# A third chunk pair of the MLP's up projection as seven block products, with four raw weight buffers in place of two and a descriptor scratch of 8 KB for GpSimd

## The chip, the cores and the metric

The kernel runs on one core of a Trainium2 chip. The metric is the device time of one execution in microseconds (us), the median of several runs. Five engines work side by side and wait for one another by semaphores: TensorE (PE, matrix products; its weight loads are listed as PEld), VectorE (DVE), ScalarE (ACT), GpSimd (POOL) and SyncE (SP), whose queue issues most of the loads here. SBUF is the working memory on the chip, PSUM the memory into which TensorE writes.

## What is computed

A trunk of two layers on a sequence of 512 positions with 1024 channels, in float32. Each layer has a wide input projection, three branches (a gated recurrence, a spatial gating unit, a windowed attention), a gated merge and an output projection, and then the part that matters here:

```python
D_FF = 4 * D_MODEL
...
        hn = rms_norm(x, ln2[l])
        x = x + jnp.square(jax.nn.relu(hn @ w_up[l])) @ w_down[l]
```

`w_up` has 1024 x 4096 elements in a layer, `w_down` 4096 x 1024.

## The kernel before

**Products in three passes.** A float32 product is made of three passes of TensorE on a shorter format: each operand is split into hi (a cast on ScalarE) and lo (the difference, on VectorE), and hi by hi, hi by lo and lo by hi are added up in PSUM. `wsplit` (L201 to L205) does that for a weight chunk of 128 x 1024: L203 on ScalarE, L204 on VectorE. The split chunks lie in `wh` and `wl`, three buffers each (`WB`). `mm3` (L207 to L210) issues the three passes. `split` (L255 to L262) is the same for other tiles: L258 on ScalarE, L259 on VectorE.

**Weights.** All weights come in chunks of 512 KB. `wload` (L179) loads one into a raw buffer `wr` by SyncE's queue (L184) and splits it; there are two raw buffers (`WR`), used all over the kernel: by the projections of the branches, the merge, the output projection and the up chunks. `uload` (L187, the load at L193) loads eight chunks of one unit into the eight `wq` buffers (`NQ`).

**The MLP.** It is cut into four quarters `qd` of 1024 hidden channels (L1244). A quarter has an up half, eight chunks `f` in four pairs `j`, and a down half. A chunk of the up half is made in one of two ways:

- directly (`proj`, L1263): 8 blocks of the contraction times three passes, 24 matmuls of 512 columns; then ReLU and square on ScalarE (L1269, L1270).
- as a pair of two chunks (`up_pair`, L493 to L544): the pair is a 2 x 2 block product, and seven products of half the size replace eight. Each of the seven has 4 blocks times three passes, 12 matmuls of 256 columns (L522 to L524), in the order 1, 2, 6, 7, 5, 4, 3. Before them VectorE makes sums of the raw weights (L499, L500, L503, L505), one of them in a PSUM tile `t2`, and four splits follow from these (three of 1024 columns, and one of 512 columns out of `t2`). After them the partial results are copied and added (L527 to L537), then ReLU and square (L538 to L543). The sums of the activations, `hx`, are made once for a layer by `left_x` (L407).

Which pairs go which way stands in two tuples, one entry for a quarter: the pairs in `PAIRS` load into `wr` (L488, L489, `ahead` False), those in `AHEAD` load into `wq` before the quarter's other work. Quarter 0 has none. Quarters 1 to 3 have pair 1 in `AHEAD` and pair 2 in `PAIRS`; pairs 0 and 3 are direct.

The result of each chunk pair is prepared for the down half, by either way: `left_first` (L360) and `left_second` (L368) with `left_sums` (L375) make splits and sums of it (L365, L382, L383, L398, and splits at L258 and L259).

The down half (`down`, L471, by `seven`, L422) is the same trick on larger blocks: seven products P1, P2, P6, P7, P5, P4, P3, each of two weight chunks with 24 matmuls of 512 columns in all at L433 to L435 (two blocks of the contraction to each chunk, two output tiles, three passes, and so 12 matmuls to a chunk). Before the products 6, 5 and 4 VectorE adds raw chunks (L447, L449, L451); after each product it adds what is in PSUM to the rows of x (L478). In front stands one more sum of raw chunks (L420). The first product takes both PSUM banks of the tag "c", one for each output tile; each pair of the up half takes one of them in turn.

**Order.** The order of the instructions on each engine is fixed when the kernel is built: a scheduler takes what is ready in its own model of time, by priority. From L831 on `hp()` raises the priority of loads, splits and sums; within that, the order of the program counts. The matmuls of TensorE may be moved against each other in this way too, within what the data allow.

**GpSimd** issues the transfers that go through DRAM: gates and merged rows that are put aside and fetched again, and the residual rows. Their descriptors lie in a scratch in SBUF, 16384 bytes of each partition unless the kernel says otherwise.

Of the kernel before, what the change touches and what calls it, by code (L numbers as in the profile page):

```python
# [59 lines left out]
def trunk(tc, xT, xt, ws, vec, fnb, bsb, snk, wst, rope, cmask, amask, ident, out):  # L60
    nc = tc.nc
# [24 lines left out]
    HOME = {t: p for p, ts in {"G": ("xs", "zt"), "Y1": ("yh",), "br": ("q", "a", "g", "ch"), "Y2": ("yi", "th"), "mlp": ("h", "xm")}.items() for t in ts}  # L86
    part = {}
    BANKS = {"m": 2, "a": 2, "c": 2, "s": 2}
    PAIRS, AHEAD = ((), (2,), (2,), (2,)), ((), (1,), (1,), (1,))
    GROUPS = (("m", "m", "c", "c"), ("a", "a", "s", "s"))  # L90
    WR, WB, NZ, NSM, NQ = 2, 3, 2, 3, 8

    CTS = {2: 5, 3: 4}

# [1325 lines left out]
```

## Time and profile before

| | us |
|---|---|
| median of 3 runs | 1645.81 |
| lowest, highest run | 1644.52, 1646.40 |
| span of the profiled execution | 1644.4 |
| first up matmul of layer 0, last of layer 1 (start) | 495.0, 1597.9 |

The mean granted clock of TensorE in the profiled execution is 0.999 of full speed. The span goes from the first to the last instruction of the program. In the lines of the profile, a group reads: line, engine, operation, written tile <- read tiles, shape, count, then the busy time, the mean in ns, and the idle time of the engine just before with what ended it. In an order of time a line reads: start in us, duration in us, engine, line, operation, and in brackets the idle time before. A matmul's duration overlaps the next one's: its pace is read from start to start.

### The profile page before, as it was taken

The numbers are of one execution on the slowest core, as the hardware profiler recorded it, in microseconds if no ns is written. First come the engines' busy times: TensorE is split into PE (matmuls) and PEld (weight loads), VectorE is DVE, ScalarE is ACT, GpSimd is POOL, SyncE is SP. The second block draws the span as 40 slices with busy tenths as digits, with TensorE's granted clock in tenths as the row PEclk, the third lists the DMA queues.
The fourth block names the chain that finished last, engine by engine and source line by source line (L and its number), as shares of the span: only waits on it lengthen the run. The fifth ranks groups of instructions, "written<-read, shape, count | busy, mean of one in ns | idle before, by whom it ended". The sixth has DMA issues, their size and how long they took to land. (4 is left out here: it accounts for less than half of the span.)

```text
span 1644.4 us, 24323 instructions
## 1 busy us (share of the span) xinstructions
PE 1631.2 (99%) x9137; PEld 1376.8 (84%) x9137; DVE 1358.9 (83%) x2183; ACT 1012.9 (62%) x1731; POOL 102.4 (6%) x165
## 2 busy tenths in 40 slices
PE   9999999999999999999999999999999999999998
PEld 7788888888888898989888888888887888989896
DVE  7888979677758988898989869887877589898887
ACT  7667567677247564646666555886862464647374
POOL 0012000000300000000010110000003000000001
PEclk9999999999999999999999999999999999999999
DMA  8343222222625333232423432223226343232311
GB/s 309 102 154 125 78 90 73 102 97 85 236 92 190 100 106 103 103 115 91 141 90 125 144 121 78 77 91 105 92 86 232 106 162 117 89 128 77 129 65 52
DMA packets 55590, 191.55 MB, mean 116 GB/s; under 512 B 7376, under 2 KB 7632, under 8 KB 55472
## 3 DMA queue, kind: packets, MB, share of 16 engines
q1 hardware_dynamic: 44352, 154.43, 27.3%
q0 software_dynamic: 10688, 35.00, 5.8%
q8 instruction: 72, 1.18, 0.3%
q10 hardware_dynamic: 432, 0.55, 0.1%
q14 instruction: 46, 0.38, 0.1%
HBM read 173.18 MB, written 16.78 MB: 116 GB/s over the span
## 5 line engine op out<-in xcount | busy, mean ns | idle before, releaser
L203 ACT CAST wh<-wq 128x1024 fp32r<-128x1024 f32 x214 | 225.2, 1053 | 205.1 <-PE dA L434 60.9
L204 DVE TENSOR_TENSOR wl<-wq,wh 128x1024 fp32r<-128x1024 f32 x214 | 260.4, 1221 | 62.8 <-ACT wh L203 60.3
L203 ACT CAST wh<-wr 128x1024 fp32r<-128x1024 f32 x164 | 172.0, 1049 | 155.1 <-PE wo L251 27.5
L204 DVE TENSOR_TENSOR wl<-wr,wh 128x1024 fp32r<-128x1024 f32 x164 | 199.9, 1220 | 61.0 <-ACT wh L203 55.1
L210 PE MATMUL up<-xh,wl 128*128 128x512 f32 x320 | 124.8, 390 | 0.0
L209 PE MATMUL up<-xl,wh 128*128 128x512 f32 x320 | 124.8, 390 | 0.0
L208 PE MATMUL up<-xh,wh 128*128 128x512 f32 x320 | 124.6, 391 | 0.0
L434 PE MATMUL dA<-wh,sh 128*128 128x512 f32 x256 | 99.8, 390 | 0.0
L433 PE MATMUL dA<-wh,sh 128*128 128x512 f32 x256 | 98.5, 390 | 0.0
L435 PE MATMUL dA<-wl,sh 128*128 128x512 f32 x256 | 91.9, 389 | 0.0
L656 DVE TENSOR_TENSOR ex<-ex 128x512 f32<-128x512 f32 x112 | 74.9, 686 | 3.5 <-ACT kt L647 3.2
L208 PEld LDWEIGHTS up<-xh,wh 128*128 128x128 f32 x320 | 60.1, 188 | 12.4
L210 PEld LDWEIGHTS up<-xh,wl 128*128 128x128 f32 x320 | 60.1, 188 | 12.3
L209 PEld LDWEIGHTS up<-xl,wh 128*128 128x128 f32 x320 | 60.1, 188 | 12.2
L644 ACT ACTIVATE qt<-ex 128x512 f32<-128x512 f32 x56 | 37.9, 677 | 33.8 <-DVE ex L656 31.8
L433 PEld LDWEIGHTS dA<-wh,sh 128*128 128x128 f32 x256 | 48.1, 188 | 10.0
L434 PEld LDWEIGHTS dA<-wh,sh 128*128 128x128 f32 x256 | 48.1, 188 | 9.9
L435 PEld LDWEIGHTS dA<-wl,sh 128*128 128x128 f32 x256 | 48.1, 188 | 9.9
L523 PE MATMUL us<-xs,wh 128*128 128x256 f32 x192 | 54.1, 283 | 0.0
L522 PE MATMUL us<-xs,wh 128*128 128x256 f32 x192 | 54.1, 283 | 0.0
L524 PE MATMUL us<-xs,wl 128*128 128x256 f32 x192 | 53.4, 283 | 0.0
L208 PE MATMUL gz<-xh,wh 128*128 128x512 f32 x128 | 50.9, 398 | 0.0
(435 smaller groups left out, 4780.6 us busy)
## 6 DMA issues: line engine op xcount, KB each, us to landing
wr<-in_ws_dram SPq DMA_DIRECT2D x158, 512.0 KB, 3.5
wq<-in_ws_dram SPq DMA_DIRECT2D x124, 512.0 KB, 4.3
thd<-zt POOLq DMA_DIRECT2D x32, 256.0 KB, 2.5
gt<-thd POOLq DMA_DIRECT2D x32, 256.0 KB, 3.9
mgd<-mg POOLq DMA_DIRECT2D x16, 256.0 KB, 2.3
mB<-mgd POOLq DMA_DIRECT2D x16, 256.0 KB, 6.7
x<-in_xT_dram SPq DMA_DIRECT2D x8, 256.0 KB, 7.5
xt<-in_xt_dram SPq DMA_DIRECT2D x8, 256.0 KB, 8.3
```

The source lines that it names most:

```text
L203: nc.scalar.copy(hi, raw)
L204: nc.vector.tensor_tensor(lo, raw, hi.bitcast(F32), ALU.subtract)
L208: nc.tensor.matmul(pt, whi, xhi, start=first, stop=False)
L209: nc.tensor.matmul(pt, whi, xlo, start=False, stop=False)
L210: nc.tensor.matmul(pt, wlo, xhi, start=False, stop=last)
L433: nc.tensor.matmul(pt, xh[:, t], hi[:, c], start=start and k == 0, stop=False, skip_group_check=True)
L434: nc.tensor.matmul(pt, xl[:, t], hi[:, c], start=False, stop=False, skip_group_check=True)
L435: return nc.tensor.matmul(pt, xh[:, t], lo[:, c], start=False, stop=k == 3, skip_group_check=True)
L522: nc.tensor.matmul(pt, hi[:, c], xh, start=n in (1, 2, 7) and k == 0, stop=False, skip_group_check=True)
L523: nc.tensor.matmul(pt, hi[:, c], xl, start=False, stop=False, skip_group_check=True)
L524: nc.tensor.matmul(pt, lo[:, c], xh, start=False, stop=k == 3, skip_group_check=True)
L656: nc.vector.tensor_tensor(o_ap, o_ap, ap_of(ex, i_, [[istep, 2]] + z), ALU.add)
```

## The change

Three constants. Pair 3 (f = 6 and 7) of quarters 1 to 3 joins pair 2 in `PAIRS`, in both layers, so that three of the four pairs of these quarters are seven-product pairs. The raw weight buffers `wr` go from two to four, for all that use them; a buffer takes 4096 bytes of each partition. The scratch for GpSimd's descriptors goes from 16384 to 8192 bytes of each partition.

```diff
-    PAIRS, AHEAD = ((), (2,), (2,), (2,)), ((), (1,), (1,), (1,))
+    PAIRS, AHEAD = ((), (2, 3), (2, 3), (2, 3)), ((), (1,), (1,), (1,))
     GROUPS = (("m", "m", "c", "c"), ("a", "a", "s", "s"))
-    WR, WB, NZ, NSM, NQ = 2, 3, 2, 3, 8
+    WR, WB, NZ, NSM, NQ = 4, 3, 2, 3, 8
...
-    nc = _bacc.Bacc("TRN2", target_bir_lowering=False, num_devices=1)
+    nc = _bacc.Bacc("TRN2", target_bir_lowering=False, num_devices=1, dynamic_dma_scratch_size=8192)
```

## The prediction

> **What bounds the kernel now.** I read the page first, then the waits of TensorE, then windows of one quarter of the MLP, and last the order of time on TensorE and VectorE in that quarter. From the page:
>
> ```profile
> span 1644.4 us, 24323 instructions
> PE 1631.2 (99%) x9137; PEld 1376.8 (84%) x9137; DVE 1358.9 (83%) x2183; ACT 1012.9 (62%) x1731; POOL 102.4 (6%) x165
> ```
>
> From the waits of TensorE, its two longest (us in total, times, longest):
>
> ```profile
> PE idle L167 <- DVE idle L164: 1.6, 1, 1.6
> PE tA L435 <- DVE wl L204: 1.3, 1, 1.3
> ```
>
> TensorE works 1631.2 of 1644.4 us and hardly ever waits; nothing else sets the end. The kernel gets shorter by as much as TensorE is given less to do, provided that whoever feeds it keeps up. The windows (core busy times PE, PEld, DVE, ACT, POOL, then clock, DMA share, GB/s): two long stretches outside the MLP, then the up half and the down half of quarter 2 of layer 1.
>
> ```profile
> 40.00:495.00 455.00, 452.86 (x2728) 378.71 (x2728) 362.01 (x654) 285.30 (x526) 43.96 (x68) 1.00 0.32 113
> 750.00:1310.00 560.00, 558.54 (x3284) 468.62 (x3283) 459.05 (x775) 366.40 (x649) 49.46 (x80) 1.00 0.33 113
> 1475.80:1517.70 41.90, 41.90 (x265) 38.06 (x264) 35.23 (x55) 26.70 (x47) 0.00 (x0) 1.00 0.29 100
> 1517.70:1556.00 38.30, 38.30 (x171) 31.71 (x169) 34.10 (x41) 17.59 (x20) 0.00 (x0) 1.00 0.34 112
> ```
>
> In the quarter TensorE has no gap (80.2 of 80.2 us), and VectorE works 35.23 + 34.10 = 69.3 us: it has 10.9 us left. The question of this case is whether the change fits into those.
>
> **What TensorE saves.** From the timeline of TensorE in this quarter: the first direct chunk pair, the first pair of seven products, its matmul number 21, the start of the down half, and a late one of its third product.
>
> ```profile
> 1475.76 0.39 PE L208 MATMUL up<-xh,wh 128*128 128x512 f32 x1
> ...
> 1486.64 0.28 PE L522 MATMUL us<-xh,wh 128*128 128x256 f32 x1
> ...
> 1489.04 0.28 PE L524 MATMUL us<-xh,wl 128*128 128x256 f32 x1
> ...
> 1517.92 0.39 PE L433 MATMUL dA<-wh,sh 128*128 128x512 f32 x1
> ...
> 1529.70 0.61 PE L435 MATMUL dA<-wl,sh 128*128 128x512 f32 x2
> ```
>
> A direct pair of chunks is 2 x 8 x 3 = 48 matmuls of 512 columns, from 1475.76 to 1486.64: 10.88 us. A pair by seven products is 7 x 4 x 3 = 84 matmuls of 256 columns; twenty of them take 1489.04 - 1486.64 = 2.40 us, so 0.120 us each and 10.08 us for the pair. Halving the columns doesn't quite halve the step, so one eighth fewer multiplications saves only 0.80 us. The change converts the fourth pair (f = 6, 7) of quarters 1 to 3 in two layers: 6 x 0.80 = **4.8 us less** on the path, if TensorE never waits.
>
> **What VectorE gets.** From its timeline in this quarter (in brackets: idle before, and what ended it):
>
> ```profile
> 1487.70 1.23 DVE L204 TENSOR_TENSOR wl<-wq,wh 128x1024 fp32r<-128x1024 f32 x1 [3.58 <-ACT wh L203]
> ...
> 1494.80 0.68 DVE L499 TENSOR_TENSOR wr<-wr,wr 128x512 f32<-128x512 f32 x1
> 1495.41 0.41 DVE L535 TENSOR_TENSOR u<-u,us 128x256 f32<-128x256 f32 x1
> 1495.74 0.68 DVE L500 TENSOR_TENSOR wr<-wr 128x512 f32<-128x512 f32 x1
> 1496.34 0.69 DVE L503 TENSOR_TENSOR t<-wr,wr 128x512 f32<-128x512 f32 x1
> ...
> 1498.14 0.69 DVE L259 TENSOR_TENSOR wl<-t,wh 128x512 fp32r<-128x512 f32 x1 [0.79 <-ACT wh L258]
> ...
> 1499.67 1.22 DVE L204 TENSOR_TENSOR wl<-wr,wh 128x1024 fp32r<-128x1024 f32 x1
> 1500.80 0.42 DVE L365 TENSOR_TENSOR sf<-u 128x256 f32<-128x256 f32 x1
> ...
> 1505.45 1.23 DVE L204 TENSOR_TENSOR wl<-wr,wh 128x1024 fp32r<-128x1024 f32 x1 [0.41 <-ACT wh L203]
> ...
> 1507.93 1.23 DVE L204 TENSOR_TENSOR wl<-wr,wh 128x1024 fp32r<-128x1024 f32 x1 [0.32 <-ACT wh L203]
> ...
> 1520.47 1.22 DVE L451 TENSOR_TENSOR wq<-wq,wq 128x1024 f32<-128x1024 f32 x1
> ...
> 1525.94 1.22 DVE L451 TENSOR_TENSOR wq<-wq,wq 128x1024 f32<-128x1024 f32 x1
> 1527.07 1.22 DVE L204 TENSOR_TENSOR wl<-wq,wh 128x1024 fp32r<-128x1024 f32 x1
> ...
> 1533.72 2.35 DVE L449 TENSOR_TENSOR wq<-wq,wq 128x1024 f32<-128x1024 f32 x2
> ...
> 1543.46 1.23 DVE L204 TENSOR_TENSOR wl<-wq,wh 128x1024 fp32r<-128x1024 f32 x1 [1.34 <-ACT wh L203]
> ...
> 1548.90 1.22 DVE L204 TENSOR_TENSOR wl<-wq,wh 128x1024 fp32r<-128x1024 f32 x1 [1.49 <-ACT wh L203]
> ```
>
> Start to start, with work waiting, a 1024-wide operation takes 1.13 us (1499.67 to 1500.80), a 512-wide one 0.60 (1495.74 to 1496.34), a 256-wide one 0.33 (1495.41 to 1495.74). A direct pair costs VectorE two splits (L204); a seven-product pair costs three, five 512-wide operations (L499, L500, L503, the split of t2 at L259, L505) and three 256-wide sums from PSUM (L529, L535, L537). The sums for the down half (L365 to L398) are needed either way. So the change adds 1.13 + 5 x 0.60 + 3 x 0.33 = **5.1 us of VectorE** to a quarter in which it has 10.9 left and TensorE takes 0.8 away: 5.0 us of 79.4 would remain.
>
> Not all of these can be used. 3.58 us lie before 1487.70: the weights of pair 1 wait there until TensorE gives back one of three split buffers. 1.34 and 1.49 lie late in the down half. What must fit is the stretch from 1487.70 to the first split of the third down product, the L204 at 1527.07 (done 1528.29):
>
> ```profile
> 1487.70:1528.30 40.60, 40.60 (x255) 36.84 (x254) 38.05 (x59) 29.50 (x50) 0.00 (x0) 1.00 0.23 78
> ```
>
> TensorE reads that split at 1529.70; it takes four hi matmuls first. So VectorE has 1529.70 - 1487.70 = 42.0 us, and after the change 41.2, for 38.05 + 5.1 = 43.2 us of work. The two L451 in this stretch can wait: they feed the sixth down product. That leaves 43.2 - 2.3 = 40.9 us, 0.3 less than there is, if VectorE never pauses. Now it pauses 40.60 - 38.05 = 2.55 us. If all of that stays, it is 40.9 + 2.55 - 41.2 = 2.2 us late; if none stays, it isn't late. So a quarter's stall lies between 0 and 2.2 us. Of the 2.55, the 0.41 and 0.32 before the splits of f = 6 and 7 go, because these splits go and the raw weights lie in four buffers; of the other 1.8 I take half, since VectorE now has a backlog to fill pauses with, but the 0.79 before the t2 split is a round trip through ScalarE and comes once more. 40.9 + 0.9 - 41.2 = **0.6 us stall in a quarter**, 3.6 in six. After this point the down half has the 1.34 and 1.49 to catch up in, and the two L451 take 2.3 of them; I add nothing there.
>
> One rule stands against a step of this sum. The row at 1533.72 has two 1024-wide additions in 2.35 us, so the second starts 0.09 before the first's 1.22 are over. The Trainium skill, page "VectorE: DVE Perf Modes", section "The DRAIN you can't avoid", has it that the next operation waits until the pipeline of the one before is empty; durations would then add whole. By it the edit costs 1.22 + 5 x 0.69 + 3 x 0.41 = 5.9 us, the stall grows by 0.8 to 1.4 us and the time to 1649.4. The row speaks for steps shorter than durations, so I give this 1 in 50, within the slower cases.
>
> **The other edits.** Four raw buffers instead of two, everywhere:
>
> ```profile
> ACT wh L203 <- DMA wr<-in_ws_dram: 19.5, 16, 5.3
> SPq L184 <- DVE wl L204: 584.1, 89, 39.2
> ```
>
> SyncE's queue waits 584 us for a raw buffer to be given back, and behind it only other loads stand; ScalarE's casts wait 19.5 us for a load. Both shrink. TensorE doesn't notice: it waits nowhere on a load, and in the two long stretches of the windows its gaps are 455.00 - 452.86 + 560.00 - 558.54 = 3.6 us altogether, mostly behind VectorE and ScalarE. I take 0, between 3.6 us gained, if all these gaps closed, and 1.3 lost, if the order of the work came out with one more wait like that of tA. In the MLP the four buffers are what makes the third pair possible: with two, pair 3 could load only when pair 2 had been split.
>
> Half the scratch:
>
> ```profile
> q0 software_dynamic: 10688, 35.00, 5.8%
> ```
>
> GpSimd's queue moves 35.00 MB, nearly all in transfers of 256 KB, so some 134 of them, and 10688 / 134 / 16 is 5 packets for each of 16 engines and transfer. The code issues eight at most in one go, 40 packets an engine. No row shows a full ring, before or at half the size; I take 0, with the price of a full one among the rivals.
>
> ScalarE gets one more 1024-wide cast, a 512-wide one and a few copies, about 3 us in a half where it works 26.70 of 41.90: hidden. The first down product needs both "c" banks of PSUM, and the last product of pair 3 now frees one of them:
>
> ```profile
> L542 ACT ACTIVATE u<-us x12: 366/382/393, 603.8 to 1589.4; 128x256 f32<-128x256 f32 x12
> ```
>
> These 382 ns, behind at most one 1024-wide cast already begun on ScalarE, hold back the products into one of the two banks; the other bank's are free to go first. I take 0, and 0.4 at worst.
>
> **The sum.** The profiled execution: 1644.4 us of span; the three runs have 1644.52, 1645.81 and 1646.40, so the median lies 1.4 above the span. 1644.4 - 4.8 + 3.6 = 1643.2, and with the 1.4 **1644.6 us**. What a measurement of this kernel can tell from no change is about 0.2%, 3.3 us: the forecast is no measurable difference, on the fast side.
>
> **The rivals.**
> *VectorE keeps up.* The pauses fill, or the order of the work is laid out so that only late-needed sums slip; no quarter stalls. For it: 5.0 us stay free in a quarter, the waiting L451 alone make the stretch balance to 0.3 us, and the hi matmuls can be drawn ahead of the lo ones. Against it: that balance leaves nothing for the round trip of the third t2. Time: 1644.4 - 4.8 + 1.4 = 1641.0. If the deeper prefetch also closed a third of the gaps outside the MLP, 1639.8.
> *VectorE becomes the bound, and the kernel is slower.* A seven-product pair costs VectorE three splits, five 512-wide and three 256-wide operations, and its sums for the down half (five 256-wide, three 512-wide): 3 x 1.13 + 8 x 0.60 + 8 x 0.33 = 10.8 us, against 10.08 on TensorE. Two such pairs run on credit, which is repaid while TensorE has the last direct pair: that costs VectorE 2 x 1.13 + 3.5 = 5.8 of 10.88 us. With a third pair the debt goes on into the down half, whose first products ask a new split of 1.13 each 2.7 us beside additions and reads of PSUM. The place is the third pair's last splits or the third down product; the price 1.9 us in a quarter if four fifths of today's pauses stay, 6 x (1.9 - 0.8) = 6.6 more than before: 1652.4. It decides from 1.35 us on (0.8 saved, and 3.3 / 6 = 0.55 beyond it). For it: before the stretch VectorE waits on a buffer, not for want of work, so the free time there can't be moved; against it, that the two L451 and the second sums of each pair are needed late.
> *The scratch is too small, and GpSimd's queue stalls.* Each time eight transfers are in flight it would wait one landing; but only loads of the merge and of the residual stand behind it, which have several us to spare. If eight such waits of 1 us reached TensorE, with the forecast's other terms: 1652.6. Nothing in the rows asks for it.
> That the pair isn't converted at all can't be: the loop asks the tuple alone.
>
> **How the numbers follow.** Forecast (stall 0.25 to 1.35 us a quarter, within 0.2%) 0.38; no stall, faster by over 0.2%, 0.35; slower by over 0.2%, 0.27, of it 0.02 for the scratch and 0.02 for the rule above. The lower end is the case without stalls, 1641.0, and half a us for gaps that close elsewhere: 1640.5. The upper end: with all of today's pauses, 2.2 us late, it is 6 x (2.2 - 0.8) = 8.4 more, 1654.2; the part of the cases above 1653 is left out.
>
> **What would show it.** Right, in the profile after: 84 matmuls of 256 columns (L522 to L524) three times in a row in quarters 1 to 3, `up` from 320 to 224 matmuls at each of L208 to L210, `us` from 336 to 504 at each of its lines; the up half 41.1 us plus its stalls; VectorE busy 31 us more in all (6 x 5.1), its free time in such a quarter near 5 us; TensorE's waits now name "wl" of L204 or L259, at the third pair or the second and third down product, 0.6 us to a quarter. Wrong: if TensorE's waits stay at a few us in all, VectorE kept up, and my pauses were too many; if they pass 8 us, or if the up half itself grows beyond 41.9 us, VectorE is the bound. A wait on a load of "wr" or on a transfer of GpSimd's queue would refute my zeros for the buffers or the scratch. The forecast also fails if steps of a stage outside the MLP move by more than 2 us.

## The result, and the profile after

The changed kernel takes 1665.51 us (median of 4 runs, 1662.89 to 1665.92). The kernel before took 1645.60 us beside it on the same chip. The ratio is 1.0119, 95% interval 1.0107 to 1.0132: slower by 1.2%. The forecast was 1644.6 with a range up to 1653.0, so it missed the sign and the range.

The page of the changed kernel: TensorE is shown busy 6.6 us longer than before, though it was given less to do. A matmul of 512 columns is drawn 0.39 us long at steps of 0.23, so the first part of each stall counts as busy, and the page's 98% hides it.

```profile
span 1664.1 us, 24841 instructions
PE 1637.8 (98%) x9353; PEld 1383.6 (83%) x9353; DVE 1388.4 (83%) x2237; ACT 1024.4 (62%) x1767; POOL 102.6 (6%) x165
```

TensorE's waits (us in total, times, longest). Three rows of the down products are new. They name ScalarE's casts of the weights (`wh`), not VectorE's differences (`wl`), which the prediction had named:

```profile
PE dC L433 <- ACT wh L203: 5.3, 5, 2.0
PE dB L433 <- ACT wh L203: 4.7, 6, 0.8
PE dA L433 <- ACT wh L203: 1.8, 6, 0.3
...
PE tA L435 <- DVE wl L204: 1.0, 2, 0.7
```

The windows of quarter 2 of layer 1 (us, then busy times of PE, PEld, DVE, ACT, POOL, clock, DMA share, GB/s), cut at the start of the down half, then whole:

```profile
1487.39:1528.60 41.21, 40.84 (x291) 38.34 (x290) 35.38 (x57) 26.09 (x47) 0.00 (x0) 1.00 0.29 98
1528.60:1570.40 41.80, 40.10 (x181) 32.54 (x181) 37.99 (x47) 20.29 (x26) 0.00 (x0) 1.00 0.30 101
```
```profile
1487.40:1570.40 83.00, 80.93 (x470) 70.88 (x469) 73.35 (x103) 46.37 (x73) 0.00 (x0) 1.00 0.30 100
```

The down half, to which the prediction added nothing, has grown from 38.3 to 41.8 us. Of these 3.5 us, 1.0 is work that changed sides (twelve matmuls of pair 3 behind the start of the down half, 1.44 us, less two down matmuls ahead of it, 0.45); the other 2.5 are waiting. VectorE has 83.00 - 73.35 = 9.65 us free in a quarter, nearly as much as before. But hardly any of it lies where the third pair's work falls. This is the same view of 47.5 us, from 22.4 us into the quarter, when pair 2 has just begun on TensorE, to the first split of the sixth down product:

```profile
1509.80:1557.30 47.50, 45.43 (x269) 39.54 (x269) 47.05 (x67) 29.91 (x48) 0.00 (x0) 1.00 0.22 72
```

VectorE works 47.05 of these 47.50 us. Its free time lies before them (3.83 us in one piece at 1499.33, ahead of a split that waits for ScalarE's cast) and after them.

The groups of the up half's matmuls (count, busy us, mean ns); the 288 and 216 of `us` make 504 for a line:

```profile
L209 PE MATMUL up<-xl,wh 128*128 128x512 f32 x224 | 87.4, 390 | 0.0
...
L523 PE MATMUL us<-xs,wh 128*128 128x256 f32 x288 | 81.2, 283 | 0.0
...
L523 PE MATMUL us<-xl,wh 128*128 128x256 f32 x216 | 60.6, 283 | 0.0
```

Where the 19.7 us of span went, from the starts of the first matmuls of each stage:

| us | before | after | buffers alone | own bank | own bank, late sums |
|---|---|---|---|---|---|
| start to first up matmul, layer 0 | 495.3 | 494.9 | 494.4 | 494.4 | 493.1 |
| quarter 0, both layers | 166.8 | 167.1 | 167.0 | 167.1 | 167.0 |
| quarters 1 and 2, both layers | 320.9 | 331.9 | 321.5 | 329.3 | 323.1 |
| quarter 3 of layer 0, to the first `tA` | 82.1 | 84.0 | 82.4 | 83.5 | 82.4 |
| seam: first `tA` to first `f` of layer 1 | 141.4 | 143.1 | 144.6 | 142.7 | 143.3 |
| from there to the up half of layer 1 | 349.5 | 349.5 | 349.5 | 349.6 | 349.5 |
| quarter 3 of layer 1, to the end | 88.4 | 93.8 | 89.8 | 90.5 | 89.8 |
| span | 1644.4 | 1664.1 | 1649.3 | 1657.0 | 1648.1 |

The columns on the right are experiments below. A quarter of the changed kind takes 82.97 us instead of 80.23: 2.7 longer, where 0.2 shorter was forecast.

### The profile page after: what moved, and what is told of

It is laid out like the page before. It is cut to its first block, busy times and chain, and to the rows that moved or that the text cites. A ratio compares the mean times of both kernels' runs of the same rounds, so it can differ in the third digit from the quotient of the medians.

```text
span 1664.1 us, 24841 instructions
## 1 busy us (share of the span) xinstructions
PE 1637.8 (98%) x9353; PEld 1383.6 (83%) x9353; DVE 1388.4 (83%) x2237; ACT 1024.4 (62%) x1767; POOL 102.6 (6%) x165
## 5 line engine op out<-in xcount | busy, mean ns | idle before, releaser
L204 DVE TENSOR_TENSOR wl<-wq,wh 128x1024 fp32r<-128x1024 f32 x214 | 259.5, 1219 | 60.8 <-ACT wh L203 58.0
L204 DVE TENSOR_TENSOR wl<-wr,wh 128x1024 fp32r<-128x1024 f32 x170 | 206.7, 1219 | 51.3 <-ACT wh L203 45.2
L209 PE MATMUL up<-xl,wh 128*128 128x512 f32 x224 | 87.4, 390 | 0.0
L210 PE MATMUL up<-xh,wl 128*128 128x512 f32 x224 | 87.4, 390 | 0.0
L208 PE MATMUL up<-xh,wh 128*128 128x512 f32 x224 | 86.6, 390 | 0.0
L524 PE MATMUL us<-xs,wl 128*128 128x256 f32 x288 | 81.1, 285 | 0.4
L522 PE MATMUL us<-xs,wh 128*128 128x256 f32 x288 | 81.2, 283 | 0.0
L523 PE MATMUL us<-xs,wh 128*128 128x256 f32 x288 | 81.2, 283 | 0.0
L522 PE MATMUL us<-xh,wh 128*128 128x256 f32 x216 | 61.8, 288 | 0.0
L523 PE MATMUL us<-xl,wh 128*128 128x256 f32 x216 | 60.6, 283 | 0.0
L524 PE MATMUL us<-xh,wl 128*128 128x256 f32 x216 | 57.3, 283 | 0.0
L524 PEld LDWEIGHTS us<-xs,wl 128*128 128x128 f32 x288 | 54.7, 191 | 1.7 <-DVE wl L204 1.7
```

What stands on the lines that cost most here:

```text
L204: nc.vector.tensor_tensor(lo, raw, hi.bitcast(F32), ALU.subtract)
L208: nc.tensor.matmul(pt, whi, xhi, start=first, stop=False)
L209: nc.tensor.matmul(pt, whi, xlo, start=False, stop=False)
L210: nc.tensor.matmul(pt, wlo, xhi, start=False, stop=last)
L522: nc.tensor.matmul(pt, hi[:, c], xh, start=n in (1, 2, 7) and k == 0, stop=False, skip_group_check=True)
L523: nc.tensor.matmul(pt, hi[:, c], xl, start=False, stop=False, skip_group_check=True)
```

## Where TensorE waits in a quarter, and for what

Each stall below is the step from one matmul's start to the next, less the usual step. In quarter 2 of layer 1 there are five of weight: 0.23 us in pair 3 and 0.46 at the first down matmul, 0.26 and 0.95 between pair 3 and the second down product, 0.99 early in the fifth. With seven smaller ones of about 0.1 us, most of them the step right behind a stall, they make 3.6 us. Before there were 0.2 in the whole quarter.

**At the hand-over of the bank.** TensorE (start, duration, then what it waited for in brackets):

```profile
1531.85 0.40 PE L435 MATMUL dA<-wl,sh 128*128 128x512 f32 x1
1533.03 0.50 PE L433 MATMUL dB<-wh,sh 128*128 128x512 f32 x1 [0.78 <-ACT wh L203]
...
1534.06 0.39 PE L433 MATMUL dA<-wh,sh 128*128 128x512 f32 x1
```

and ScalarE beside it:

```profile
1531.93 1.04 ACT L203 CAST wh<-wq 128x1024 fp32r<-128x1024 f32 x1 [0.78 <-PE us L523]
1532.88 0.38 ACT L542 ACTIVATE u<-us 128x256 f32<-128x256 f32 x1
```

P1 has two output tiles in the two "c" banks. The second bank comes free only when L542 has read pair 3's last product, at 1533.26. So the order on TensorE puts the second product (`dB`) ahead of most of P1's second tile, and its cast has to wait for a split buffer that pair 3 still reads (`us` L523).

**In the down half.** VectorE, five rows out of a stretch of work with one pause of 0.45 us:

```profile
1535.96 1.22 DVE L451 TENSOR_TENSOR wq<-wq,wq 128x1024 f32<-128x1024 f32 x1
...
1541.24 1.22 DVE L451 TENSOR_TENSOR wq<-wq,wq 128x1024 f32<-128x1024 f32 x1
...
1549.62 1.21 DVE L449 TENSOR_TENSOR wq<-wq,wq 128x1024 f32<-128x1024 f32 x1
...
1551.41 1.21 DVE L449 TENSOR_TENSOR wq<-wq,wq 128x1024 f32<-128x1024 f32 x1
...
1553.87 3.48 DVE L204 TENSOR_TENSOR wl<-wq,wh 128x1024 fp32r<-128x1024 f32 x3
```

L449 makes the weights of the fifth product P5, L451 those of the sixth, P4. VectorE does both L451 first, 8 to 14 us ahead of the L449 that is due earlier. P4's first split is only the last of the three in the row at 1553.87. This order is not new: in the kernel before, the rows of the prediction at 1520.47, 1525.94 (L451) and 1533.72 (L449) show the same, and no product waited. New is that VectorE has hardly a pause left to make up for it. ScalarE's cast of P5's second chunk then has to wait for the second L449, and the cast behind it, the second one in this row, for its turn:

```profile
1552.73 2.00 ACT L203 CAST wh<-wq 128x1024 fp32r<-128x1024 f32 x2 [0.74 <-DVE wq L449]
```
```profile
1554.78 0.50 PE L433 MATMUL dC<-wh,sh 128*128 128x512 f32 x1 [0.83 <-ACT wh L203]
```

`dC` is the tile of P7 and P4, and P7 is over by then: TensorE is given four matmuls of P4 ahead of the rest of P5, and waits for the cast that ends at 1554.73. So the wait points at ScalarE, but this cast stood behind one that was itself waiting for a sum of VectorE. A releaser in such a row is the last link only; the rows before it in time tell the cause.

## Experiments

Two theories stood at first: VectorE has too much to do (amount), or single things are in the wrong place (the bank, the buffers, the order). "Quarter" below is quarter 2 of layer 1, start to start: 80.2 before, 82.97 after. (In most kernels quarters 1 and 2 of both layers agree within 0.2 us.) Ratios are to the kernel before on the same chip, with 95% intervals.

**The parts alone.** First the memory edits without the third pair, and later the scratch by itself.

```diff
-    PAIRS, AHEAD = ((), (2, 3), (2, 3), (2, 3)), ((), (1,), (1,), (1,))
+    PAIRS, AHEAD = ((), (2,), (2,), (2,)), ((), (1,), (1,), (1,))
```

> Four raw buffers and half the scratch, with pairs 1 and 2 as before and pair 3 direct. Theory load (VectorE's 5.1 us more in a quarter are the cause, wherever the third pair stands) and theory seam (the pair that stands next to the down half holds one of the two c banks and the split buffers that the first down products need): both the time of before, 1645.6, within 2 us. Theory buffers (the two memory edits cost by themselves, through another order of the work or through GpSimd's queue): 1650 or more.

Measured: 1651.05 us, 1.0040 (1.0025 to 1.0054); quarter 80.38. It is slower with no further pair converted. The quarters are nearly untouched; the table has 3.2 us at the seam of the layers and 1.4 at the end. TensorE there, in this kernel:

```profile
826.61 0.60 PE L330 MATMUL xT<-id_t,xr 128*128 128x128 f32 x4
828.04 0.80 PE L330 MATMUL xT<-id_t,xr 128*128 128x128 f32 x4 [0.84 <-ACT xf L335]
830.35 0.96 PE L208 MATMUL bu<-xh,wh 128*128 128x512 f32 x3 [1.50 <-ACT xh L258]
```

and in the kernel before:

```profile
824.82 0.60 PE L330 MATMUL xT<-id_t,xr 128*128 128x128 f32 x4
...
827.10 0.60 PE L330 MATMUL xT<-id_t,xr 128*128 128x128 f32 x4
827.45 1.18 PE L208 MATMUL bu<-xh,wh 128*128 128x512 f32 x4
```

Before, the transposes (`xT`) were strewn among the `tA` matmuls; with four buffers the last ones stand in a row, with nothing between them and the `bu` products that need them. Nothing waits on a load there: the buffers changed the order that the scheduler lays out, not the traffic.

```diff
-    nc = _bacc.Bacc("TRN2", target_bir_lowering=False, num_devices=1)
+    nc = _bacc.Bacc("TRN2", target_bir_lowering=False, num_devices=1, dynamic_dma_scratch_size=8192)
```

> The kernel before with half the scratch, and nothing else. Theory scratch (GpSimd's queue is held up): some of the 6.4 us that the two memory edits cost together, 1647 or more. Theory order (four raw buffers make the scheduler lay out the work differently at the seam of the layers and in the tail): no difference from before, 1644.7 within 1.5.

Measured: 1646.24 us, 1.0002 (0.9993 to 1.0012); quarter 80.17. Half the scratch costs nothing; by subtraction, what the memory edits cost is the order with four raw buffers. (Four raw buffers with the full scratch were not run.)

Then the pair without the memory (two raw buffers, the full scratch):

```diff
-    WR, WB, NZ, NSM, NQ = 4, 3, 2, 3, 8
+    WR, WB, NZ, NSM, NQ = 2, 3, 2, 3, 8
...
-    nc = _bacc.Bacc("TRN2", target_bir_lowering=False, num_devices=1, dynamic_dma_scratch_size=8192)
+    nc = _bacc.Bacc("TRN2", target_bir_lowering=False, num_devices=1)
```

> Pairs 1, 2 and 3 by seven products with two raw buffers and the full scratch. Load and seam: no faster than the changed kernel's 1665.5, and slower by as much as pair 3's loads come late (they can start only when pair 2 is split, and land some 4 us later): 1666 to 1680. Buffers: clearly faster than 1665.5, near 1650.

Measured: 1671.52 us, 1.0161 (1.0146 to 1.0176); quarter 84.8. The third pair needs its raw buffers: without them a quarter is 1.8 us longer still.

**Another pair in place of the last.** Pair 0 is converted and pair 3 stays direct:

```diff
-    PAIRS, AHEAD = ((), (2, 3), (2, 3), (2, 3)), ((), (1,), (1,), (1,))
+    PAIRS, AHEAD = ((), (0, 2), (0, 2), (0, 2)), ((), (1,), (1,), (1,))
```

> Pairs 0, 1 and 2 by seven products and pair 3 direct, the rest as in the changed kernel: the same work on every engine, only the place of the direct pair differs. Load: near the changed kernel, 1661 to 1668. Seam: TensorE's stalls at the start of the down half go, 1641 to 1650.

Measured: 1662.98 us, 1.0109 (1.0094 to 1.0124); quarter 82.33. The same loss in another place: the two largest stalls are now 1.31 us at an L522 and 0.86 at an `up` L208, both behind ScalarE's casts and within the up half. With a direct pair last, the down half is not where TensorE waits. The time is the one that the amount theory had named; what follows parts the two.

**A bank of its own.** Pair 3's first accumulator goes into an "s" bank, so that P1 finds both "c" banks free:

```diff
-    def up_pair(r0, r1, hx, bank):
+    def up_pair(r0, r1, hx, bank, first="c"):
...
-        pc, pm, pa = (PT(b, "us")[:, 0:HT] for b in ("c", bank, "a"))
+        pc, pm, pa = (PT(b, "us")[:, 0:HT] for b in (first, bank, "a"))
...
-... "s" if j % 2 else "m")
+... "s" if j % 2 else "m", "s" if j == 3 else "c")
```

> The changed kernel with the first partial results of pair 3 in a bank of tag s in place of c, so that both c banks are free when the down half starts. Load: within 2 us of 1665.5. Seam: the wait at the first products of the down half goes, about 1.2 us in each of six quarters, 1655 to 1660; if the bank is all of it, 1645.

Measured: 1658.93 us, 1.0083 (1.0068 to 1.0098); quarter 82.33. The 0.26 and 0.95 are gone, yet the quarter gains only 0.64. The down half takes the rest back: TensorE comes through the hand-over 1.2 us sooner and then stalls 1.12 us at the start of the fourth product (`dC`) and 0.64 at the start of the fifth (`dA`), in place of the 0.99. The fourth waits for a cast, the fifth for VectorE's reading of the bank (L478); ahead of both, VectorE has done the two L451. TensorE's waits are now these:

```profile
PE dC L433 <- ACT wh L203: 5.7, 6, 1.0
PE dA L433 <- DVE xr L478: 3.0, 5, 1.1
PE dA L433 <- ACT wh L203: 1.7, 6, 0.3
```

The experiments that follow are built on this one, unless they say otherwise.

**More split buffers, or raw buffers of its own.**

```diff
-    WR, WB, NZ, NSM, NQ = 4, 3, 2, 3, 8
+    WR, WB, NZ, NSM, NQ = 3, 4, 2, 3, 8
...
-    nc = _bacc.Bacc("TRN2", target_bir_lowering=False, num_devices=1, dynamic_dma_scratch_size=8192)
+    nc = _bacc.Bacc("TRN2", target_bir_lowering=False, num_devices=1, dynamic_dma_scratch_size=4096)
```

> The kernel with pair 3's own bank, with four buffers for split weights in place of three (three raw buffers and a scratch of 4096 bytes pay for it). Load: the same work for VectorE, which only may start a little earlier; a quarter 81.3 to 82.5, 1652 to 1659. Split buffers: the quarter comes near 79.5, 1641 to 1647.

Measured: 1682.36 us, 1.0222 (1.0207 to 1.0237); quarter 82.6. A fourth split buffer doesn't cure the quarter, and from the start of quarter 3 of layer 0 to the up half of layer 1 it takes 591.1 us, where the run with the bank alone took 575.8. But it changes where the quarter stalls: the 0.23 and 0.46 in pair 3 and at P1 are gone, in all four of quarters 1 and 2, and 1.85 us stand in their place at the second product, behind a cast of ScalarE (`sh`, L258), beside 1.07 at the fourth. So those 0.7 us seem to come with three split buffers, though the time of the quarter alone doesn't show it. (The order of the work differs in this run, and so do the raw buffers and the scratch, so it isn't shown by itself.)

```diff
-    WR, WB, NZ, NSM, NQ = 4, 3, 2, 3, 8
+    WR, WB, NZ, NSM, NQ = 2, 3, 2, 3, 8
...
-... name=nm("wq")) if ahead else sb.tile([P, CW], F32, tag="wr", bufs=WR, name=nm("wr"))
+... name=nm("wq")) if ahead else sb.tile([P, CW], F32, tag=tag, bufs=2, name=nm("wr"))
...
+pair_load(keys(j), False, "wp" if j == 3 else "wr")
```

> The kernel with pair 3's own bank, and with pair 3's raw weights in two buffers of their own, so that the rest of the kernel has two raw buffers as before. Order: the stretch from the first t product of layer 1 to its first gate projection comes back from 142.7 to near 141.4 us of before and the tail shortens; 1654 to 1657, with the quarters as they are (82.3). If the four buffers cost nothing but by chance, 1657 to 1660.

Measured: 1661.20 us, 1.0092 (1.0077 to 1.0107), above both of the expected ranges; quarter 82.31, the same as with four for all. The seam is back at 142.0 us, but the MLP of layer 0 begins 4 us later (498.4), with a wait of 2.8 us of `bu` behind ScalarE's `wh` of L258, 8.55 us into the program. This time a load is the cause. SyncE's queue, and ScalarE behind it:

```profile
0.74 0.86 SPq L489 DMA_DIRECT2D wr<-in_ws_dram  x2
1.65 0.42 SPq L753 DMA_DIRECT2D x<-in_xT_dram  x1
```
```profile
7.27 0.72 ACT L261 ACTIVATE xh<-x,vec_t 128x512 fp32r<-128x512 f32 x1 [4.60 <-DMA x<-in_xT_dram]
7.90 1.17 ACT L258 CAST wh<-wr 128x512 fp32r<-128x512 f32 x2
```

Pair 3's own buffers (L489) are free from the start, so two of its loads go out ahead of the first load of `x`, which the run with the bank alone issues at 0.74.

**Less for VectorE in the down half.** Sums are left out (so that the down products take other weights): the early one (L420) and P4's (L451) in quarters 1 to 3; then all four kinds.

```diff
-                    elif n == 4:
+                    elif n == 4 and not less:
...
-                    if f == 3:
+                    if f == 3 and not PAIRS[qd]:
```

> The kernel with pair 3's own bank, without two kinds of sums of raw down weights (L420 and L451) in quarters 1 to 3, so that the down products are of other weights than the reference's; four operations of 1.13 us on VectorE less in a quarter, 4.5 of the 5.1 that the third pair added. TensorE's work is unchanged. Load: its stalls nearly go, a quarter of 82.3 comes to 79.5 to 80.5, and the time to 1643 to 1649. Theory split buffers (three buffers for split weights are too few, and TensorE waits for casts that wait for a buffer): the quarter stays above 81.5, 1655 or more.

Measured: 1648.53 us, 1.0023 (1.0013 to 1.0032); quarter 80.37. Four operations fewer, 4.5 us of VectorE, take 2 us off the quarter: the down half is clean. That, too, is what the amount theory had named.

```diff
-                    if n == 6:
+                    if n == 6 and not less:
...
-                    elif n == 5:
+                    elif n == 5 and not less:
```

> The kernel with pair 3's own bank, without any of the sums of raw down weights (L420, L447, L449, L451) in quarters 1 to 3, so that the down products are of other weights than the reference's; VectorE has 9.0 us less in a quarter, nearly twice what the third pair added. Load: the 0.95 us of stalls that stayed when half of this was left out go as well where they come from a backlog, a quarter of 79.5 to 80.0, 1641 to 1646. If they come from the pairs' own round trips (VectorE's 10.8 us against 10.08 within the three pairs), the quarter stays at 80.4, 1648.

Measured: 1649.24 us, 1.0025 (1.0014 to 1.0036); quarter 80.39. Another 4.5 us less gain nothing. By amount alone the second half should have helped too, at least with the stalls of 0.23 and 0.45 that remain in pair 3 and at P1.

**The same sums on GpSimd**, first L420 and L451, then all four kinds:

```diff
-                nc.vector.tensor_tensor(b12, b12, b22, ALU.add)
+                (eng or nc.vector).tensor_tensor(b12, b12, b22, ALU.add)
...
-                        V.tensor_tensor(b21[i], b21[i], b11[i], ALU.add)
+                        (nc.gpsimd if pool else V).tensor_tensor(b21[i], b21[i], b11[i], ALU.add)
```

> The kernel with pair 3's own bank, with the sums of raw down weights at L420 and L451 on GpSimd in place of VectorE in quarters 1 to 3: VectorE has four operations of 1.13 us less in a quarter, as where they were left out. Load: a quarter of about 80.4 and 1647 to 1651, if GpSimd makes a sum in less than some 8 us and doesn't slow VectorE. If VectorE is slowed while GpSimd works, or the sums come late, the quarter stays at 82 or goes above it, 1657 or more.

> As the last, with the sums at L447 and L449 on GpSimd too: eight operations of 1.13 us less on VectorE in a quarter, and each of these sums stands right ahead of a split that a down product waits for. Load, with a sum on GpSimd below 3 us: a quarter of 79.5 to 80.4, 1641 to 1648. With a slower GpSimd the down products wait for their sums, 1655 or more.

Measured: 1674.18 us, 1.0175 (1.0160 to 1.0190), quarter 84.05; and 1702.33 us, 1.0343 (1.0327 to 1.0358), quarter 88.7. Of the first, GpSimd's groups (count, busy us, mean ns), the longest wait of TensorE, and one split on VectorE while a GpSimd sum runs:

```profile
L420 POOL TENSOR_TENSOR wq<-wq,wq 128x1024 f32<-128x1024 f32 x12 | 37.2, 3118 | 261.3 <-DMA wq<-in_ws_dram 261.3
L451 POOL TENSOR_TENSOR wq<-wq,wq 128x1024 f32<-128x1024 f32 x12 | 34.8, 2899 | 268.1 <-DVE wl L204 268.1
```
```profile
PE dA L434 <- DVE sh L259: 11.9, 6, 2.0
```
```profile
1497.91 2.11 DVE L204 TENSOR_TENSOR wl<-wq,wh 128x1024 fp32r<-128x1024 f32 x1
```

GpSimd isn't a way out: it takes 2.9 to 3.1 us for a sum of 1.22, and VectorE's own splits beside it grow.

**More for VectorE, without the third pair.** The kernel with the memory edits alone gets 5.1 us of idle work on VectorE (a maximum of a raw chunk with itself) ahead of the splits of f = 6 and 7 in quarters 1 to 3:

```diff
+            for _ in range(min(busy, 2)):
+                nc.vector.tensor_tensor(raw, raw, raw, ALU.max)
+            if busy > 2:
+                nc.vector.tensor_tensor(raw[:, 0:S], raw[:, 0:S], raw[:, 0:S], ALU.max)
...
+                        w = wload(l, "up", qd, f, busy=(f - 4) * (PAIRS[qd] != () and f > 5))
```

> Four raw buffers and half the scratch with pair 3 direct, and 5.1 us of VectorE work that changes nothing (a maximum of a tile with itself) put ahead of the splits of f = 6 and 7 in quarters 1 to 3. TensorE's work, the banks and the split buffers are those of the kernel with the buffers alone, which took 1651.0 with quarters of 80.4. Load: the quarters grow by 1 to 2.6 us, 1657 to 1667. If it takes the products, banks or buffers of the third pair, the quarters stay at 80.4, 1649 to 1653.

Measured: 1652.78 us, 1.0052 (1.0035 to 1.0069); quarter 80.41, against 80.38 without the load. The windows of the whole quarter, of its down half and of the 47.5 us from 22.4 us into the quarter on:

```profile
1480.10:1560.50 80.40, 80.40 (x434) 69.74 (x432) 74.15 (x100) 44.29 (x67) 0.00 (x0) 1.00 0.32 106
...
1522.10:1560.50 38.40, 38.40 (x171) 31.64 (x169) 36.65 (x45) 18.43 (x22) 0.00 (x0) 1.00 0.34 116
```
```profile
1502.50:1550.00 47.50, 47.50 (x244) 40.57 (x244) 43.58 (x59) 28.81 (x43) 0.00 (x0) 1.00 0.27 90
```

VectorE works 74.15 of 80.40 us, more and denser than in the changed kernel (73.35 of 83.00), and TensorE has no gap at all. The amount in a quarter does not make TensorE wait. But the run has less in the tight stretch: 43.58 of 47.50 us, against 47.05. What as much work would do there, without the third pair, it doesn't show. P4's sums stand ahead of P5's here too (L455 and L453 in this kernel), without harm:

```profile
1525.45 1.22 DVE L455 TENSOR_TENSOR wq<-wq,wq 128x1024 f32<-128x1024 f32 x1
...
1539.18 1.22 DVE L453 TENSOR_TENSOR wq<-wq,wq 128x1024 f32<-128x1024 f32 x1
```

**The place of one sum.** What was open then: why four sums fewer help when 5.1 us more do no harm. In this kernel nothing is left out; the two L451 are tied behind both L449 on VectorE, in quarters 1 to 3.

```diff
-                        V.tensor_tensor(t3[i], b11[i], b22[i], ALU.subtract)
+                        m5 = V.tensor_tensor(t3[i], b11[i], b22[i], ALU.subtract)
...
-                        V.tensor_tensor(b21[i], b21[i], b11[i], ALU.add)
+                        with behind(m5 if late else None):
+                            V.tensor_tensor(b21[i], b21[i], b11[i], ALU.add)
```

> Beside e4_own_bank, which it is but for this: in quarters 1 to 3 the two sums behind P4's weights (L451) are put behind both sums of P5's weights (L449) on VectorE; no work is left out. E4 took 82.33 us a quarter and 1658.93 in all. Theory of the place in the order (the two L451 run some 13 us before P4's splits need them and push what is due earlier back): the two stalls of the down half, 1.11 and 0.64 us in e4, go for the most part, so 80.6 to 81.2 us a quarter, 6 x 1.1 to 1.7 less, 1649 to 1652 in all. Theory of the amount (VectorE simply has too much in the half): the stalls move to a later product and stay about 1.7 us, 82.1 to 82.5 a quarter, 1657 to 1660.

Measured: 1651.33 us, 1.0035 (1.0022 to 1.0048); quarter 80.76. The same work in another order takes 1.57 us off the quarter. VectorE now (L451 is L452 here):

```profile
1535.72 1.21 DVE L449 TENSOR_TENSOR wq<-wq,wq 128x1024 f32<-128x1024 f32 x1
...
1540.44 1.22 DVE L449 TENSOR_TENSOR wq<-wq,wq 128x1024 f32<-128x1024 f32 x1
1541.58 2.35 DVE L452 TENSOR_TENSOR wq<-wq,wq 128x1024 f32<-128x1024 f32 x2
```

and the window of the same 47.5 us:

```profile
1500.00:1547.50 47.50, 47.05 (x280) 41.42 (x279) 47.17 (x68) 30.99 (x49) 0.00 (x0) 1.00 0.24 78
```

From the start of the quarter (1477.6) the first L449 ends after 59.3 us; in the changed kernel (start 1487.4) after 63.4. VectorE is as full as there, 47.17 of 47.50 us, and TensorE hardly waits. Of its waits on `dC` and `xr` one row of 0.4 us is left, and one of 0.4 on a split (`wl`) is new:

```profile
PE dA L433 <- ACT wh L203: 1.7, 6, 0.3
...
PE dC L433 <- DVE xr L479: 0.4, 1, 0.4
...
PE dA L435 <- DVE wl L204: 0.4, 1, 0.4
```

Two controls take away equal amounts of VectorE's work, 2.4 us each, at two places:

```diff
-                    elif n == 4:
+                    elif n == 4 and not less:
```

> E4_own_bank with the two sums behind P4's weights (L451) left out in quarters 1 to 3, so that P4 multiplies with other weights than the reference's: 2.4 us less for VectorE a quarter. Theory of the place: most of what leaving out all four sums gained (82.33 to 80.37) comes back, 80.4 to 81.0 us a quarter, 1648.5 to 1652. Theory of the amount: half of it, 81.2 to 81.6 a quarter, 1653 to 1655.

```diff
-                    if f == 3:
+                    if f == 3 and not PAIRS[qd]:
```

> E4_own_bank with the two early sums of the down weights (L420) left out in quarters 1 to 3, so that the down products take other weights than the reference's: 2.4 us less for VectorE a quarter, ahead of the down half. Theory of the place (they run ahead of P1, not between the late splits): 81.9 to 82.4 us a quarter, 1656 to 1659. Theory of the amount: half of the gain of leaving out all four, 81.2 to 81.6 a quarter, 1653 to 1655.

Measured: without L451 1649.05 us, 1.0022 (1.0012 to 1.0031), quarter 80.37; without L420 1658.43 us, 1.0080 (1.0065 to 1.0095), quarter 82.41. Equal amounts, 2.0 us and nothing. Leaving L451 out gains only 0.39 more than moving it. That settles place against amount for this part: in a stretch in which VectorE has hardly a pause, what counts is how much of its work stands ahead of an operation that is due. The scheduler lays out the other engines anew around the moved sums, so the 1.57 us are the worth of the whole order that comes with their place, not of the two rows by themselves.

**The place alone, and with raw buffers of its own.** The same tie in the changed kernel itself, with the bank as it was:

> The changed kernel itself (the fourth pair's first accumulator still in the bank of the tile before) with the two sums behind P4's weights (L451) put behind P5's (L449) on VectorE in quarters 1 to 3; no work is left out. The changed kernel took 82.97 us a quarter, 82.33 with the bank alone changed, 80.77 with bank and place changed. If bank and place are two causes that add: 82.97 less 1.56, 81.3 to 81.5 us a quarter, 1654 to 1657 in all. If the place alone is the cause and the bank only gave slack to it: 80.7 to 81.0 a quarter, 1650 to 1653. If the place decides only once the bank is free: 82.3 to 83.0, 1659 to 1666.

Measured: 1661.50 us, 1.0099 (1.0082 to 1.0116); quarter 82.59. The bank alone is worth 0.64 us in a quarter, the place alone 0.38, both together 2.21. The third of the cases that were written down, then: the place decides only once the bank is free. The four times fit this reading: while TensorE loses 1.2 us at the hand-over, VectorE catches up in that time, and an order that is too slow by about as much shows little. In this run the 0.25 and 0.95 at the bank are still there, and 0.57 in the down half in place of 0.99.

And in the kernel with two raw buffers for all and two for pair 3:

> E8_own_raw (two raw buffers for all, two more for the fourth pair alone; 82.31 us a quarter, 1661.2 in all, of which 4 were a later start of the MLP) with the same change of place of L451. Theory of the place: 6 x 1.1 to 1.7 us less, 1651 to 1654.6; if the order outside the MLP also comes out as in the kernel before, down to 1647. Theory of the amount: 1660 to 1662.

Measured: 1653.01 us, 1.0046 (1.0030 to 1.0063); quarter 80.81. The quarter gains 1.5 us here too; the late start stays (496.7 us to the first up matmul). No version here beats the kernel before.

## Why the prediction was wrong, point by point

- **TensorE's saving: right to 0.1 us.** `us` has 504 matmuls a line and `up` 224, as forecast. In the kernel with bank and place mended a quarter of 80.76 us has stalls of 1.4, so 79.3 without them; before, 80.23 less 0.2 is 80.0. That is 0.7 saved, against 0.80.
- **VectorE's extra work: right within 5%.** 1388.4 - 1358.9 = 29.5 us, forecast 31. By the rule that the prediction cites from the Trainium skill ("VectorE: DVE Perf Modes", "The DRAIN you can't avoid") durations would have added whole. The row at 1541.58 of the run with late sums has two additions in 2.35 us, where one takes 1.22. The same section of the Trainium skill adds that a next operation that is not held starts earlier, and the row agrees with that.
- **The stall up to P6's first split (0.6 us): the size near, the place in part, and so in part luck.** At P6 itself nothing waits. The 0.23 in pair 3 end with VectorE's split (`wl`), out of a row of work without a pause, as the prediction had it; the 0.46 at P1 end with a cast of ScalarE, which it had not. Both stand, to 0.02, in each of the runs whose quarter was taken apart step by step with three split buffers and pair 3 converted (bank, less for VectorE, late sums), and with four they are gone.
- **"I add nothing there", of the down half: the step that failed first.** "The two L451 in this stretch can wait", the budget said. They could have waited, but the order was laid out when the kernel was built, and they do not: they stand at 1535.96 and 1541.24, ahead of P5's sums, as in the prediction's own rows from before. The budget took the best order for the one that would come, and ended at P6's first split, which did come about on time. The bill came later: 0.99 us, and 1.76 once the bank no longer hid it. With the two L451 behind L449, 0.24 of it is left.
- **The "c" bank, "I take 0, and 0.4 at worst": failed.** 0.26 + 0.95 us in a quarter. The 382 ns of L542 were seen, and also a cast ahead of them; that TensorE would be given P2 first, whose split buffer pair 3 still held, was not.
- **The four raw buffers, 0 (at worst 1.3): failed.** By themselves they cost 5 to 6 us (the run with the memory edits is 4.9 us of span longer, the scratch adds none), 4.6 of it in the order at the seam and the end. ScalarE's wait on loads of `wr` did go, from 19.5 us in all to the row below; SyncE's did not shrink, as claimed, but grew from 584.1. Neither was on the path.

```profile
ACT wh L258 <- DMA wr<-in_ws_dram: 0.4, 1, 0.4
```
```profile
SPq L184 <- DVE wl L204: 605.2, 87, 39.2
```

- **The scratch, 0: right**, 1.0002 (0.9993 to 1.0012).
- **The rival "VectorE becomes the bound": right in sign, half right in mechanism.** Its argument holds: the debt does go on into the down half, where VectorE has hardly a pause left, and the free time ahead of the stretch stays unused. It set the price at 1.9 us of stall in a quarter and 1652.4 (four fifths of the pauses give 1.7 by the prediction's own sum); a quarter stalls 3.6. But 1.2 of these are the bank's, and the run with late sums has VectorE just as full and loses only 0.24 us in the down half: there it is the order that costs, not the load alone.
- The six quarters together: forecast -0.2 each, measured +2.7. Of the 19.7 us, 11.0 lie in quarters 1 and 2 of both layers, 1.9 in quarter 3 of layer 0, 5.4 from quarter 3 of layer 1 to the end, and 1.7 at the seam. The prediction's own mark for stages outside the MLP, 2 us, was passed by the seam of the kernel with the memory edits alone (3.2).

**What stays open:** whether a fourth split buffer beside the late sums would clear the whole quarter (the two were not run together), and what in the scheduler moves the work at the seam and the end by some 3 us with four raw buffers. With the bank and the place mended, a quarter stands at 80.76: 0.7 saved, 1.2 more lost than before.

## What to carry to other kernels

An engine's free time over a stage says little when it lies where the new work can't use it; write down for each of its operations when it is due, to the end of the stage, and ask of each that "can wait" whether the order that is laid out makes it wait. When work takes over a bank or buffer from other work, look at which product is put first instead and whether its own inputs are ready. And where a scheduler lays out the order, try the memory edits alone: they can cost more than the work that they make room for.

## What the runs showed of the hardware

In the run with L420 and L451 on GpSimd, a sum of 128 x 1024 float32 values takes GpSimd 2899 to 3118 ns in the mean, where VectorE takes 1.22 us; and while it runs, VectorE's differences of two tiles grow, from 1.22 to 2.11 us in the row above. The 24 splits (L204) that overlap such a sum take 2.15 us in the mean, the other 361 take 1.22. The Trainium skill ("SBUF — State Buffer", "Who interferes with whom") has it that a VectorE instruction with two SBUF inputs contends with a GpSimd instruction that reads SBUF; the rows agree.
